# Ten instead of eight heads of an output projection in seven products, two weight sums spread over the pair stage, and the last store on a second queue

## The chip, the cores and the metric

The kernel runs on one core of a Trainium2 chip. The metric is the device time of one execution in microseconds (us), the median of several runs. Engines are named as the profile names them: PE multiplies matrices (PEld loads its weights), DVE is the vector engine, ACT the scalar engine, POOL the GpSimd engine, and SP issues most of the transfers.

## The reference

One layer of a hybrid decoder trunk over 16 meta tokens and 512 tokens of width 2048. The normalised input goes through one projection; its columns feed six gated DeltaNet heads, five GLA heads and five forgetting-attention ("fox") heads, all 128 wide on the value side. The gated head outputs are put side by side (768 + 640 + 640 = 2048) and go through one output projection, then the residual and a final RMSNorm:

```
o_fox = o_fox.reshape(fz.shape) * jax.nn.silu(fz)
o = jnp.concatenate([o_dn, o_gla, o_fox], axis=-1)[:, PAD:].astype(x.dtype)
return x + o @ w_out
...
return rms_norm(h, final_norm_w)[:, N_META:]
```

The change concerns `x + o @ w_out`: 512 tokens, sixteen heads of 128 as the inner dimension, 2048 columns. Everything is float32.

## The kernel before

**Precision.** A float32 product is made of three products of rounded parts: each operand is split into a high part (a cast on ACT, L165 for weights, L1360 and L1370 for activations) and a low part (a subtraction on DVE, L166 for weights, L624 for activations). So each block of a product takes three matmuls: high by high, high by low, low by high. A load of 128x1024 weights (512 KB) is done by `load_half`: a transfer into a `raw` buffer (L147), then the split into `whi` and `wlo`. Two buffers of each rotate.

**Order.** The program is written with a scheduler that orders each engine's instructions ahead of the run by a simulated time and by priorities; on the chip each engine then works through its list in order. A dependency marked `NoSync` only orders the lists; one marked `Sync` also makes the instruction wait on the chip. The weight splits have the highest priority. `paced(x)` lets `x` follow the latest weight split in the order, without a wait.

**Stages.** (1) Input projection of the DeltaNet, GLA and first fox columns, with the token mixers between its matmuls. (2) The *pair stage*: for the last fox heads two column blocks at a time are projected by seven products (`inproj_pair`, L571, seven weight loads for each of seven pairs), with the attention of the preceding head between them (scores L1219 and L1220, softmax L1223 to L1234, transposes L1237, values L1267 to L1271). (3) The output projection (`mms`, matmuls at L1392), which also hides the attention of the last fox head (head 4).

**Output projection.** The heads are numbered 0 to 15: six DeltaNet, five GLA, five fox. The first `SH` = 8 are taken in four pairs. A pair is a 2 x 2 product: two halves of the tokens by two heads, times two heads by two halves of the columns. It is done by seven products of half size instead of eight, in the way of Strassen and Winograd. The seven operands of a pair are `a11`, `a12`, `s2`, `s1`, `s3`, `s4` and `a22`, each 128 x 512 with its two heads' token halves summed as needed. `first_sums` makes `s1` and `s3` on POOL (L634, L635), `differences` (L1434) and L1464 make `s2` and `s4` on DVE, and `operand` splits each one into its high and low part. One operand of one pair needs one load of 512 KB of weights and 12 matmuls of 128x512. Four of the seven weights are sums of blocks of `w_out`, held in DRAM in `tw`. The other `NP` = 8 heads (`plain`) are multiplied in the usual way, in twos: `run` takes two heads and 512 columns, with one load and 24 matmuls.

The order of stage 3 is:

- `pa`: for three blocks of 512 columns (`cc` 0 to 2), the first `EARLY` = `NP - 2` plain heads, `EARLY // 2` runs per block. Between the runs one entry at a time is taken from a list of steps: splitting the plain heads' outputs (`split_o`, from `zrow` or a `zp` row), `load_zr` (L1345, the pairs' outputs from DRAM), `first_sums`, then the operands. `begin` loads x into the accumulators `acc` through POOL's queue (L1386).
- the seven products, `pq`, `pr`, `ps`, over all pairs in turn, on four PSUM banks each. The first uses the pool `psb`, the second the pool `psm`, which the last fox head's attention uses too. `take` adds the results to `acc` on DVE (L1407).
- `pt`: the last two plain heads for `cc` 0 to 2, the first two of the last block's six (`LAST` = `NP - 6` = 2) in one more run, and then, token block by token block, six plain heads of the last column block with weights loaded beforehand by `load_last` (`wl`). After each token block follow the norm, the scaling by row (L1577 on ACT for `cc` 0 and 2, L1579 and L1581 on DVE) and four stores of 256 KB each (L1582).

**Chores.** The summed weights for the pair stage (`ti`) and for the output projection (`tw`) are made by transfers from DRAM to DRAM on POOL's queue: a plain copy (L492) or an accumulating copy (L490). They stand in a list `chores`, each `yield`ing a cost of 1 for a copy and 1.6 for a sum. Every `load_half` adds `rate` to `due` and takes chores while `due` is above zero. One entry of `AHEAD` sets the rate to 1.4 and enters seven groups of jobs for `ti`, and behind them the groups for `tw`, one per pair of heads:

```
AHEAD = {(0, -1): (1.4, (-1, -2, -3, -4, -5, -6, -7), (0, 1, 2, 3))}
...
due[0] += rate[0]
while due[0] > 0 and chores:
    cost = next(chores[0], None)
```

A group has four copies and four sums; for several groups, all copies come first, then the first two sums of each group (into `tw[j, 0]` and `tw[j, 2]`), then the third of each (`tw[j, 1]`), then the fourth of each (`tw[j, 3]`). `fetch` (called after products of the last pair) brings the plain heads' outputs from DRAM into `zrow`.

Of the kernel before, what the change touches and what calls it, by code (L numbers as in the profile page):

```python
# [14 lines left out]
ALU = mybir.AluOpType  # L15
# [3 lines left out]
P = 128  # L19
# [11 lines left out]
LOW = -87.0  # L31

DN_HEADS, GLA_HEADS, FOX_HEADS = 6, 5, 5
SH = 8
NK = 8
H1 = 1
SKIP = 1
# [45 lines left out]
def tile_hybrid_trunk(ctx, tc, xT, xtok, mtok, w_gate, w_in, w_out, w_dn, consts, lmask, fin_w, out, dbg=None):  # L83
    nc = tc.nc
# [12 lines left out]
    def row(name, dt=F32):  # L97
        return wk.tile([P, 3 + T], dt, tag="row", bufs=7, name=name)
# [4 lines left out]
    V, A, G, PE = nc.vector, nc.scalar, nc.gpsimd, nc.tensor  # L103
# [66 lines left out]
    pace, splits, heads_, waits = [None, None], [], [], []  # L170

    def paced(*ins):

        for x in ins:
            tc.add_manual_dep(x.ins, pace[x.ins.engine == pace[1].engine].name, mybir.DependencyInfo(
                mybir.DependencyClass.NoSync, mybir.DependencyReason.DATA), reason="paced")
# [16 lines left out]
    def part(name, n=512):  # L193
        return hp.tile([P, T], F32R, tag="x", name=name)[:, :n]
# [29 lines left out]
    head = {}  # L224
# [254 lines left out]
    ti = drp.tile([len(PAIRS), 4, P, KC], F32, name="ti")  # L479
    tw = drp.tile([SH // 2, 4, P, 1024], F32, name="tw")  # L480
    zd = drp.tile([DN_HEADS + GLA_HEADS + FOX_HEADS - 1, P, S], F32, name="zd")
# [3 lines left out]
    def steps_of(jobs):  # L485

        nonlocal ready
        for kind, out_, in_ in jobs:
            if kind:
                paced(G.dma_start(out=out_, in_=in_, accum_op=ALU.add, max_dma_last_dim=2048))  # L490
            else:
                x = G.dma_start(out=out_, in_=in_)  # L492
                paced(x)
                if ready < 4:
                    ready += 1
                    tc.add_manual_dep(x.ins, maxes[0].name, mybir.DependencyInfo(
                        mybir.DependencyClass.NoSync, mybir.DependencyReason.DATA), reason="behind")
            yield 1.6 if kind else 1
# [14 lines left out]
    def jobs(*groups):  # L513

        for st in range(4):
            for g_ in groups:
                chores.append(steps_of(g_[st]))
# [85 lines left out]
    def conv_silu(key, blk, dst, meta=True):  # L603
# [8 lines left out]
        for w in range(1, 4):  # L612
# [9 lines left out]
             + [("fz", h) for h in range(FOX_HEADS)])  # L622
    heads = heads[:SH] + heads[11 : 11 + F1] + heads[SH:11] + heads[11 + F1 :]
    sub = lambda o, a, b: V.tensor_tensor(out=o, in0=a, in1=b, op=ALU.subtract)  # L624
    pairs = range(SH // 2)
    t0, t1 = slice(0, 256), slice(256, 512)
# [515 lines left out]
            V.memset(first_[n][:, 0:1], 0.0)  # L1142

    def fetch(i):
        if i < 6:
            if i % 3 == 0:
                zrow.append(six.tile([P, 3, S], F32, tag="six", name=f"zp{i}"))
            paced(nc.sync.dma_start(out=zrow[-1][:, i % 3], in_=zd[SH + i]))

# [123 lines left out]
            nc.sync.dma_start(out=zd[DN_HEADS + GLA_HEADS + h], in_=z)  # L1273


    AHEAD = {(0, -1): (1.4, (-1, -2, -3, -4, -5, -6, -7), (0, 1, 2, 3))}
    XSUM = {1: (0, 1, 2), 2: (3, 4, 5), 3: (6, 7)}
    MIX = 10
    PM, SP = (308, 340), (8, 11)
# [1 line left out]
    def ahead(g, i):  # L1281
        for n in AHEAD.get((g, i), ()):
            if isinstance(n, tuple):
                jobs(*[in_jobs(-k - 1) if k < 0 else out_jobs(k) for k in n])
            else:
                rate[0] = n
# [52 lines left out]
    def load_zr():  # L1339

        for i in range(SH):
            if i % 2 == 0:
# [3 lines left out]

    plain = heads[SH:]
    NP = len(plain)
    EARLY, LAST = NP - 2, NP - 6
    oparts = {}  # L1350

    def split_o(i):
        z = zs[plain[i]]
        if i < 6:
            z = zrow[i // 3][:, i % 3]
        elif i < NP - 1:
            z = row(f"zp{i}")[:, :S]
            nc.sync.dma_start(out=z, in_=zd[SH + i])
        hi, lo = part(f"oh{i}"), part(f"ol{i}")
        made = A.copy(hi, z), sub(lo, z, hi.bitcast(F32))  # L1360
        if i > 1:
            paced(*made)
        oparts[i] = hi, lo
# [26 lines left out]
    def mms(p_, o, w, s, first, last):  # L1390
        for n, (o_, w_) in enumerate(((o[0], w[0]), (o[0], w[1]), (o[1], w[0]))):
            mm = PE.matmul(p_, o_[:, s], w_, start=(first and n == 0), stop=(last and n == 2), skip_group_check=True)  # L1392
            order.append(mm.ins)
# [11 lines left out]
    def add(tb, cc, p_, c=slice(0, 512), op=ALU.add):  # L1405
        a = acc[tb, cc][:, c]
        V.tensor_tensor(out=a, in0=a, in1=p_[:, c], op=op)  # L1407
# [4 lines left out]
    def square(tb, cc, c=slice(0, 512), n=0):  # L1412
        sq = row(f"sqf{tb}{cc}{n}")
        A.activation(sq[:, c], acc[tb, cc][:, c], AF.Square, accum_out=ss[:, tb, cc + n : cc + n + 1])  # L1414
# [16 lines left out]
    def differences():  # L1431
        for j in pairs:
# [3 lines left out]
            r["s2"] = r["a11"]  # L1436

    rest = lambda a, b: [split_o(i) for i in range(a, b)]
    steps = [lambda a=a: rest(a, min(a + 2, EARLY)) for a in range(2, EARLY, 2)] + [load_zr]
    steps.append(lambda: (first_sums(), rest(EARLY, EARLY + 1)))  # L1440
# [85 lines left out]
    for c in range(4):  # L1526
        f = part(f"fw{c}").bitcast(F32)
# [20 lines left out]
    for tb in range(4):  # L1548
        cuts = 2 if tb == 3 else 1
        for n in range(cuts):  # L1550
            c = slice(0, 512) if cuts == 1 else slice(CUT, 512) if n else slice(0, CUT)
            p_ = psm.tile([P, 512], F32, tag="m", name="pz") if n else pa[tb]
            for i in range(LAST, NP):
                mms(p_[:, c], oparts[i], [t[:, c] for t in wl[i]], slice(tb * P, (tb + 1) * P),
                    (n == 1 or LAST == 0) and i == LAST, i == NP - 1)
            add(tb, 3, p_, c)
            if n < 1:
                square(tb, 3, c, n)
                if tb == 3:
                    r = rr[:, tb : tb + 1]  # L1560
                    V.reduce_sum(r, ss[:, tb, :4], axis=mybir.AxisListType.X)
                    V.tensor_scalar(r, r, 1.0 / D, EPS, ALU.mult, ALU.add)
        r = rr[:, tb : tb + 1]
        if tb < 3:
            V.reduce_sum(r, ss[:, tb, :4], axis=mybir.AxisListType.X)
            V.tensor_scalar(r, r, 1.0 / D, EPS, ALU.mult, ALU.add)
        else:
            a = acc[tb, 3][:, c]
            V.tensor_tensor_reduce(out=row("sqz")[:, c], in0=a, in1=a, scale=1.0 / D, scalar=r, op0=ALU.mult,
                                   op1=ALU.add, accum_out=rr[:, 4:5])  # L1570
            r = rr[:, 4:5]
        A.activation(r, r, AF.Ln)
        A.activation(r, r, AF.Exp, scale=-0.5)
        for cc in (0, 1, 2, 3):
            a = acc[tb, cc]
            if cc % 2 == 0:
                A.activation(a, a, AF.Copy, scale=r)  # L1577
            elif cc == 3:
                V.scalar_tensor_tensor(out=a, in0=a, scalar=r, in1=fw[cc], op0=ALU.mult, op1=ALU.mult)  # L1579
            else:  # L1580
                V.tensor_scalar_mul(a, a, r)  # L1581
            nc.sync.dma_start(out=out[tb * P : (tb + 1) * P, cc * 512 : (cc + 1) * 512], in_=a)  # L1582


def _layout(x, meta_tokens, norm_w, w_in, conv_w, a_log, dt_bias, dn_norm_w, w_gk2, b_gk,
# [57 lines left out]
```

## Time and profile before

| What | Value |
|---|---|
| median of three runs (lowest, highest) | 1000.51 us (999.34, 1000.78) |
| the profiled execution: its time, its span | 997.56 us, 995.9 us |
| granted PE clock, mean | 0.997 |
| instructions | 19769 |
| POOL busy | 249.0 us, 25% |
| moved by DMA | 186.05 MB, mean 187 GB/s |

Busy times are sums over the span. Matmuls overlap each other in the pipeline, so that the duration of one (about 0.39 us for 128x512) is longer than its share of the time; the spacing is read from a chain or from the start times of a row of them. In the chain of waits, a row is: start, length, what. In groups of instructions the two numbers behind the bar are busy time in us and the mean of one in ns. In the timeline, the brackets give the idle time before an instruction and what ended it.

### The profile page before, as it was taken

The numbers are of one execution on the slowest core, as the hardware profiler recorded it, in microseconds if no ns is written. First come the engines' busy times: TensorE is split into PE (matmuls) and PEld (weight loads), VectorE is DVE, ScalarE is ACT, GpSimd is POOL, SyncE is SP. The second block draws the span as 40 slices with busy tenths as digits, with TensorE's granted clock in tenths as the row PEclk, the third lists the DMA queues.
The fourth block names the chain that finished last, engine by engine and source line by source line (L and its number), as shares of the span: only waits on it lengthen the run. The fifth ranks groups of instructions, "written<-read, shape, count | busy, mean of one in ns | idle before, by whom it ended". The sixth has DMA issues, their size and how long they took to land.

```text
span 995.9 us, 19769 instructions
## 1 busy us (share of the span) xinstructions
PE 980.4 (98%) x7774; PEld 896.6 (90%) x7774; DVE 666.8 (67%) x1443; ACT 475.3 (48%) x1043; POOL 249.0 (25%) x293
## 2 busy tenths in 40 slices
PE   9999999999999999999999999999999999999996
PEld 7899999899999888899999988799999998888885
DVE  6356786966567895434675847776766676877573
ACT  7653533334456234334546444555555554454353
POOL 0031423322233244301313223221221134000060
PEclk9999999999999999999999999999999999999998
DMA  9754666777547688844847866565454577355634
GB/s 346 263 193 168 210 216 238 172 181 173 116 113 169 140 215 198 298 130 144 209 143 190 186 178 178 176 200 161 168 172 135 182 267 273 106 190 199 202 106 169
DMA packets 67489, 186.05 MB, mean 187 GB/s; under 512 B 13725, under 2 KB 16973, under 8 KB 66692
## 3 DMA queue, kind: packets, MB, share of 16 engines
q1 hardware_dynamic: 41920, 121.86, 36.0%
q0 software_dynamic: 16576, 56.83, 23.9%
q10 hardware_dynamic: 8900, 6.10, 2.2%
q8 instruction: 61, 1.00, 0.4%
q14 instruction: 32, 0.26, 0.1%
HBM read 174.07 MB, written 56.69 MB: 232 GB/s over the span
## 4 chain that ended last, share of the span: by engine, by line
PE 70%; DVE 7%; DMA 5%; ACT 3%; issue 2%; POOL 1%; ACTq 0%; DVEq 0%; POOLq 0%
PE pp L240 28%; PE pp_a L571 8%; PE pa L1392 5%; PE pq L1392 4%; PE pt L1392 4%; PE ps L1392 2%; PE pp_b L571 2%; PE pp_d L571 2%; PE pp_c L571 2%; DVE wlo L166 2%; DMA sc<-ab 1%; DMA zd<-gqk 1%; PE pr L1392 1%; PE pss L1041 1%; ACT whi L165 1%
## 5 line engine op out<-in xcount | busy, mean ns | idle before, releaser
L240 PE MATMUL pp<-xh,wlo 128*128 128x264 f32 (+2 forms) x1120 | 272.9, 306 | 2.2 <-DVE wlo L166 2.2
L240 PE MATMUL pp<-xh,whi 128*128 128x264 f32 (+2 forms) x1120 | 273.9, 306 | 0.0
L240 PE MATMUL pp<-xl,whi 128*128 128x264 f32 (+2 forms) x1120 | 272.9, 306 | 0.0
L165 ACT CAST whi<-raw 128x1024 fp32r<-128x1024 f32 x131 | 137.1, 1047 | 157.0 <-PE pp L240 81.2
L166 DVE TENSOR_TENSOR wlo<-raw,whi 128x1024 fp32r<-128x1024 f32 x131 | 160.6, 1226 | 72.8 <-ACT whi L165 64.2
L240 PEld LDWEIGHTS pp<-xh,wlo 128*128 128x128 f32 x1120 | 182.6, 189 | 12.1 <-DVE wlo L166 3.6
L240 PEld LDWEIGHTS pp<-xh,whi 128*128 128x128 f32 x1120 | 182.6, 189 | 9.4 <-ACT whi L165 0.4
L240 PEld LDWEIGHTS pp<-xl,whi 128*128 128x128 f32 x1120 | 182.7, 189 | 8.9 <-issue 0.4
L385 POOL TENSOR_SCALAR stc<-cv 128x528 f32<-128x528 f32 (+1 forms) x18 | 28.9, 1607 | 144.9 <-DVE cv L613 124.4
L613 DVE SCALAR_TENSOR_TENSOR cv<-pb,cpk,cv 128x528 f32<-128x528 f32 (+1 forms) x54 | 41.1, 761 | 0.8
L1417 POOL TENSOR_TENSOR acc<-acc,fw 128x512 f32<-128x512 f32 x4 | 5.8, 1483 | 117.4 <-ACT sqf L1414 117.4
L571 PE MATMUL pp_a<-t,whi 128*128 128x264 f32 (+1 forms) x224 | 30.5, 284 | 0.0
L1392 PE MATMUL pa<-wloo,oh 128*128 128x512 f32 x72 | 28.7, 398 | 0.0
L571 PE MATMUL pp_a<-xh,whi 128*128 128x264 f32 x112 | 28.4, 288 | 0.0
L571 PEld LDWEIGHTS pp_a<-t,whi 128*128 128x128 f32 x224 | 27.9, 189 | 0.5
L1392 PE MATMUL pa<-whio,ol 128*128 128x512 f32 x72 | 28.4, 394 | 0.0
L571 PE MATMUL pp_a<-xl,whi 128*128 128x264 f32 x112 | 28.3, 287 | 0.0
L385 POOL TENSOR_SCALAR stdz<-zdz 128x512 f32<-128x512 f32 x6 | 11.3, 1885 | 62.1 <-DVE zdz L403 62.0
L165 ACT CAST whis<-raws 128x1024 fp32r<-128x1024 f32 x16 | 16.3, 1048 | 21.2 <-PE pq L1392 10.8
L166 DVE TENSOR_TENSOR wlos<-raws,whis 128x1024 fp32r<-128x1024 f32 x16 | 19.2, 1223 | 10.7 <-ACT whis L165 10.6
L1392 PE MATMUL pa<-whio,oh 128*128 128x512 f32 x72 | 26.0, 400 | 0.0
L740 DVE TENSOR_TENSOR ab<-ab 51x30 f32<-51x30 f32 (+14 forms) x60 | 21.2, 354 | 6.4 <-DMA ab<-scr 4.2
(509 smaller groups left out, 2138.6 us busy)
## 6 DMA issues: line engine op xcount, KB each, us to landing
raw<-in_w_in SPq DMA_DIRECT2D x103, 512.0 KB, 3.7
ti<-in_w_in POOLq DMA_DIRECT2D x42, 512.0 KB, 5.5
raw<-ti SPq DMA_DIRECT2D x28, 512.0 KB, 3.3
tw<-in_w_dn POOLq DMA_DIRECT2D x24, 512.0 KB, 5.9
ti<-ti POOLq DMA_DIRECT2D x14, 512.0 KB, 6.3
rawo<-in_w_out SPq DMA_DIRECT2D x13, 512.0 KB, 3.2
raws<-tw SPq DMA_DIRECT2D x12, 512.0 KB, 3.9
xt<-in_xtok SPq DMA_DIRECT2D x8, 512.0 KB, 8.9
```

What stands on the lines that cost most here:

```text
L165: pace[0] = A.copy(hi, raw).ins
L166: pace[1] = V.tensor_tensor(out=lo, in0=raw, in1=hi.bitcast(F32), op=ALU.subtract).ins
L240: mm = PE.matmul(p_[:, :nt], wt[:, j * m : (j + 1) * m], xx[k][:, t0 : t0 + nt], start=(k == 0 and wt is hi and xx is xh), stop=(k == KT - ...
L385: maxes.append(G.tensor_scalar_max(t, src, LOW).ins)
L571: m = PE.matmul(p_[:, cols], wt[:, j * P : (j + 1) * P], xx[j][part_][:, cols], start=first and i == 0, stop=i == len(todo) - 1, skip_grou ...
L613: V.scalar_tensor_tensor(out=c, in0=pb[:, t0 + w : w + T], scalar=cwc[:, blk, w : w + 1], in1=c, op0=ALU.mult, op1=ALU.add)
L740: V.tensor_tensor(out=t3, in0=a3[:, j + 1 :, j : j + 1].to_broadcast([NN * 4 + H, m, j]), in1=a3[:, j : j + 1, 0:j].to_broadcast([NN * 4 + ...
L1041: mm = PE.matmul(ps[o0 : o0 + n, b * n : b * n + n], kx[rr, k0 : k0 + n], qx[rr, q0 : q0 + n], start=True, stop=True)
L1392: mm = PE.matmul(p_, o_[:, s], w_, start=(first and n == 0), stop=(last and n == 2), skip_group_check=True)
L1417: G.tensor_tensor(out=acc[tb, cc], in0=acc[tb, cc], in1=fw[cc], op=ALU.mult)
```

## The change

`SH` goes from 8 to 10: five pairs of heads go by seven products, and six heads remain plain (`NP` = 6, `EARLY` = 4, `LAST` = 0). With that:

- `fetch` brings four heads' outputs instead of six, and `split_o` takes those four from `zrow`.
- The groups for `tw` get a fifth pair, and from the second fox head on the rate falls to 0.35. A sum that is issued in the pair stage gets a `Sync` dependency on the latest weight split on DVE, so POOL waits for it on the chip.
- The four column blocks of a token block are scaled and stored in the order 1, 0, 3, 2, and the very last store (token block 3, `cc` 2) goes through ACT's queue instead of SP's.

```diff
-SH = 8
+SH = 10
...
         for kind, out_, in_ in jobs:
             if kind:
-                paced(G.dma_start(out=out_, in_=in_, accum_op=ALU.add, max_dma_last_dim=2048))
+                x = G.dma_start(out=out_, in_=in_, accum_op=ALU.add, max_dma_last_dim=2048)
+                if ("pair", 0) in head:
+                    tc.add_manual_dep(x.ins, pace[1].name, mybir.DependencyInfo(
+                        mybir.DependencyClass.Sync, mybir.DependencyReason.DATA), reason="paced")
+                else:
+                    paced(x)
...
     def fetch(i):
-        if i < 6:
+        if i < 14 - SH:
...
-    AHEAD = {(0, -1): (1.4, (-1, -2, -3, -4, -5, -6, -7), (0, 1, 2, 3))}
+    AHEAD = {(0, -1): (1.4, (-1, -2, -3, -4, -5, -6, -7), (0, 1, 2, 3, 4)), ("f", 1): (0.35,)}
...
     def split_o(i):
         z = zs[plain[i]]
-        if i < 6:
+        if i < EARLY:
             z = zrow[i // 3][:, i % 3]
...
-        for cc in (0, 1, 2, 3):
+        for cc in (1, 0, 3, 2):
             a = acc[tb, cc]
...
-            nc.sync.dma_start(out=out[tb * P : (tb + 1) * P, cc * 512 : (cc + 1) * 512], in_=a)
+            (nc.scalar if tb == 3 and cc == 2 else nc.sync).dma_start(
+                out=out[tb * P : (tb + 1) * P, cc * 512 : (cc + 1) * 512], in_=a)
```

## The prediction

> **What bounds the kernel now.** I read the page first (engine shares, DMA issues), then PE's waits, then the chain of waits from the last pair product to the end.
>
> ```profile
> PE 980.4 (98%) x7774; PEld 896.6 (90%) x7774; DVE 666.8 (67%) x1443; ACT 475.3 (48%) x1043; POOL 249.0 (25%) x293
> ```
>
> PE's waits from 600 us to the end (total, times, longest):
>
> ```profile
> PE pp L240 <- DVE wlo L166: 0.5, 1, 0.5
> PE pss L1041 <- DVE kq L1027: 0.4, 2, 0.2
> ```
>
> The chain, some pieces (start, length):
>
> ```profile
> 814.39 0.13 PE pfa L1219 x2
> ...
> 845.90 12.06 PE pa L1392 x52
> ...
> 869.32 0.46 PE pfo L1270 x2
> 869.78 1.16 PE pa L1392 x5
> 870.94 11.12 PE pq L1392 x48
> ...
> 948.43 37.73 PE pt L1392 x168
> ```
>
> PE waits 0.9 us in the last 396 us, and the whole output projection is PE behind PE. So a matmul taken out is worth its spacing, as long as nothing else becomes late. A 128x512 matmul takes 12.06/52 = 0.232 us in `pa` and 11.12/48 = 0.232 us in the products. In `pt` 96 of them lie between these starts:
>
> ```profile
> 948.27 1.10 PE L1392 MATMUL pt<-whio,oh 128*128 128x512 f32 x4
> ...
> 970.38 0.40 PE L1392 MATMUL pt<-wlh,oh 128*128 128x512 f32 x1
> ```
>
> That is 22.11/96 = 0.230 us.
>
> **Matmuls: -2.7 us.** `pa` goes from nine runs to six: 72 matmuls less, -16.7 us. Seven products get a fifth pair: 84 more, +19.5 us. `pt` loses the run before the last column block: 24 less, -5.5 us. The last token blocks keep their six heads. Together 12 fewer and -2.7 us. All of it lies on PE's path.
>
> **Splits: 0.** Loads of weights (`pa`, products, `pt` with `load_last`) go from 9 + 28 + 7 = 44 to 6 + 35 + 6 = 47.
>
> ```profile
> L165 ACT CAST whis<-raws 128x1024 fp32r<-128x1024 f32 x16 | 16.3, 1048 | 21.2 <-PE pq L1392 10.8 <-PE ps L1392 6.2 <-PE pr L1392 4.2
> L166 DVE TENSOR_TENSOR wlos<-raws,whis 128x1024 fp32r<-128x1024 f32 x16 | 19.2, 1223 | 10.7 <-ACT whis L165 10.6
> L1370 ACT CAST s<-zr 128x256 fp32r<-128x256 f32 x16 | 6.2, 403 | 3.4 <-DVE zr L1434 2.4 <-PE pq L1392 0.5 <-PE pr L1392 0.4
> L624 DVE TENSOR_TENSOR s<-zr,s 128x256 fp32r<-128x256 f32 x16 | 6.3, 420 | 0.0
> L624 DVE TENSOR_TENSOR ol<-zp,oh 128x512 fp32r<-128x512 f32 x7 | 7.6, 1114 | 0.0
> L1407 DVE TENSOR_TENSOR accs<-accs,pq 128x512 f32<-128x512 f32 x12 | 7.8, 682 | 0.0
> ```
>
> A load in a product has 12 x 0.232 = 2.8 us of PE beside it and needs 1.05 us of ACT and 1.22 us of DVE; one operand of one pair adds 0.40 and 0.42 us, and four `take`s of 0.68 us are now shared by five loads instead of four. That is 1.22 + 0.42 + 0.54 = 2.2 us of DVE per 2.8 us, against 2.3 before: PE still covers it. Without that cover each split would cost up to 2.3 us. The casts wait for PE in that row, not PE for them.
>
> **The `pa` stage: 0 to +2.3 us, I take +0.2.** It is here that the cover gets thin. Five stretches of the stage, only the first and their sum:
>
> ```profile
> 814.84:826.00 11.16, 11.16 (x52) 9.15 (x52) 8.64 (x23) 4.69 (x10) 9.12 (x14) 1.00 0.99 351
> ...
> sum 56.10, PE 56.10 PEld 45.88 DVE 41.68 ACT 23.40 POOL 18.74; mean PE 11.22 PEld 9.18 DVE 8.34 ACT 4.68 POOL 3.75
> ```
>
> Of 56.1 us, 216 x 0.232 = 50.1 are `pa` and 6.0 the last head's attention. With 144 the stage lasts 33.4 + 6.0 = 39.4 us and ends at 854.2. DVE had 41.7 us of work there; three splits (-3.7) and two subtractions of plain heads (-2.2) go, two operands (+0.8) and one difference (+0.4) come: 37.0 us in 39.4. But six `s` subtractions (2.5) and the four L1464 (1.4) have until the second product, so 33.1 us must be done, 84%.
>
> The attention is the piece that can be late: it ran from 814.4 to 869.8 (the chain above), and one more DVE step freed its bank at 870.5:
>
> ```profile
> 869.81 0.69 DVE L1271 TENSOR_TENSOR zfz<-pfo,zfz 128x512 f32<-128x512 f32 x1 [1.55 <-PE pfo L1270]
> ```
>
> Now `a11` starts at 854.2 and ends 60 x 0.232 = 13.9 us later, 868.1. The next product needs all four `psm` banks, its fourth bank 9 matmuls (2.1 us) after its start. If the attention keeps its old end, PE waits 870.5 - 870.2 = 0.3 us where the other three banks are free, 2.4 us where the late bank comes first. The scheduler places the attention's steps ahead of operands, so I take 0.2.
>
> Transfers stay: 15 loads of `zp` and `zr` before (7 + 8), 15 after (5 + 10), two of them shifted into the busy stretch above (0.99 of the DMA engines). The first adds need x in `acc`:
>
> ```profile
> 816.66 2.24 POOL L1386 DMA_DIRECT2D acc<-in_xtok  x4
> ...
> DMA to landing us min/median/max: 5.8/7.2/7.6
> ```
>
> The last of four lands at about 818.4 + 7.6 = 826.0. Before, 72 matmuls came ahead of the adds; now 48, and PE asks for the first freed bank at 814.8 + 48 x 0.232 + 0.5 of attention = 826.4, for the fourth 2.1 us later. Two loads more at 351 GB/s are 1.5 us, so 827.5 + 0.7 for the add: just covered, at worst 0.5 us late.
>
> POOL makes two more sums (L634, L635):
>
> ```profile
> 830.23 2.13 POOL L634 TENSOR_TENSOR zr<-zr 128x256 f32<-128x256 f32 x3
> 833.80 2.13 POOL L635 TENSOR_TENSOR zr<-zr 128x256 f32<-128x256 f32 x3
> 833.89 3.67 DVE L166 TENSOR_TENSOR wloo<-rawo,whio 128x1024 fp32r<-128x1024 f32 x1
> ```
>
> A split beside three such sums took 3.67 instead of 1.22 us, 0.8 us per sum. So two sums may cost DVE 1.6 us, and runs of 5.6 us cover that.
>
> **Weight sums in the pair stage: 0, at worst +7.** Costs in the list: seven groups for `ti` at 10.4 (4 + 4 x 1.6) are 72.8, four for `tw` 41.6, together 114.4; five make it 124.8. The loads:
>
> ```profile
> raw<-in_w_in SPq DMA_DIRECT2D x103, 512.0 KB, 3.7
> raw<-ti SPq DMA_DIRECT2D x28, 512.0 KB, 3.3
> tw<-tw POOLq DMA_DIRECT2D x8, 512.0 KB, 7.4
> ```
>
> 131 loads, 49 of them in the pair stage, leave 82 before it: 82 x 1.4 = 114.8. That took all of the old list; of the new one six sums are left (one into `tw[4, 1]`, five into `tw[j, 3]`). At 0.35 one goes per 4 to 5 loads, so they are through after about 24 of 49, long before the products read `tw`. The four copies and two first sums of the fifth pair go at the old rate among the earlier ones, between matmuls of a PE that is 98% busy over the span; I count them at 0, and at the price of the six below if that cover fails.
>
> In the pair stage there was no such traffic. Landings of `raw` there (first fence), and from 592 to 640 us, with sums beside them (second):
>
> ```profile
> DMA to landing us min/median/max: 3.1/3.3/6.7
> ```
>
> ```profile
> DMA to landing us min/median/max: 3.3/4.7/7.1
> ```
>
> Room, from a split and its product:
>
> ```profile
> 805.03 1.05 ACT L165 CAST whi<-raw 128x1024 fp32r<-128x1024 f32 x1 [0.89 <-DMA raw<-ti]
> ...
> 808.70 2.94 PE pp_c L571 x24
> ```
>
> This cast waited 0.89 us for its transfer and still ended 2.6 us ahead. A sum must delay a load by more than that; the medians differ by 1.4. I take 0.
>
> The wait that the change adds stands in POOL's list; behind it queue the scalings (L1181, L1186, L1187), the masks (L1207) and the silu's L385, which the attention needs, and through it PE. POOL already stood 21.2 us at such a split without PE waiting:
>
> ```profile
> POOL fqk L1207 <- DVE wlo L166: 21.2, 2, 17.1
> L490 POOL DMA_DIRECT2D tw<-tw x8: 879/1003/1642, 557.3 to 618.3; - x8
> ```
>
> One issue holds POOL 1.0 us, six times in 170 us.
>
> **Last stores: -0.3 (0 to -0.5).**
>
> ```profile
> 990.04 0.70 ACT L1577 ACTIVATE accs<-accs,frs 128x512 f32<-128x512 f32 x1
> 990.83 0.89 SPq L1582 DMA_DIRECT2D out<-accs  x2
> ...
> L1582 SPq DMA_DIRECT2D out<-accs x12: 332/399/1793, 977.7 to 991.3; - x12
> DMA to landing us min/median/max: 2.7/3.1/4.0
> ```
>
> The last store (`cc` 2) has its tile at 990.74, but SP begins to issue it at 991.3, as the second of that pair. ACT can begin at 990.75, 0.5 us earlier, and then SP's store of 990.8 is last. The new order 1, 0, 3, 2 is the one in which SP already issued them as they came ready, so by itself it moves nothing. If the transfers, not the issues, set the end, the gain is 0. From the row alone it might also be more: landings reach 4.0 us where 2.7 would do, and if SP's own queue made that difference, a second queue would save up to 1.3 us besides. I take -0.3, nearest to the issue's own 0.4, and 0 and -0.5 for the ends.
>
> The Trainium skill ("DMA: Bandwidth & Descriptors", Issuing engines are not separate DMA queues) says that transfers issued from different engines end on the same 16 DMA engines, so that a second issuer saves only the time of issuing. By it nothing of the 1.3 us comes back and the sum would stand at -0.4 for this part at most; no run so far has two issuers for these stores, so the trace cannot yet say.
>
> **Sum.** -2.7 + 0.2 - 0.3 = -2.8 us. The profiled execution took 997.6 us, its span 995.9 and 1.7 around it; it becomes 994.8. It stood 2.9 below the median of the runs, 1000.5, for which I forecast 997.7.
>
> **Rivals.**
>
> *The attention keeps its end and PE waits at the bank change.* For it: the attention's pace is set by DVE, not by PE's share. Against: 84% is not full, and its steps go ahead of operands in the order. With 2.4 instead of 0.2: -0.6 us, 999.9, no measurable change.
>
> *DVE becomes the bound of the shorter `pa` stage.* In the last block of the attention, between the exponential and the scaling of its result, lie these:
>
> ```profile
> 849.04 0.19 ACT L1229 ACTIVATION_READ_ACCUMULATOR fp<-fp,fsm 128x1 f32 x1
> ...
> 855.17 0.48 DVE L1234 TENSOR_SCALAR fp<-fp,fsm 128x512 f32<-128x512 f32 x1
> ```
>
> 5.9 us went to operands and adds queued between. Operands now come earlier, into the blocks before it. If one more block loses 5.9 us, the attention ends at 876.4, PE waits 876.4 - 870.2 = 6.2 us at the bank change, and the net is -2.7 - 0.3 + 6.2 = +3.2: 1003.7. It is slower by over 0.2% from an end at 875.2 on. Against: the order is planned anew, and 33 us of needed work fit.
>
> *The thin sums delay the pair stage.* If all six make a load land in 7.1 instead of 3.3 us, 3.8 less the room of 2.6 is 1.2 us each, 7.2 in all: +4.4, 1004.9. It decides when landings pass 5.9 us. Against: most room is larger, and a sum meets two or three loads only.
>
> *The second queue gives nothing* is the end 0 of that term, inside the forecast.
>
> **How the numbers follow.** A measurement of this kernel tells about 0.2%, 2.0 us, from no change. Forecast 0.60, bank change 0.18, DVE 0.14, sums 0.08. Faster by over 0.2% (below 998.5) is the forecast, 0.60; within, the bank change, 0.18; slower, the other two, 0.22. The forecast's own range is 996.5 to 998.5: its terms give -3.2 to -2.0, and below that 0.8 for the spread of the runs. With the bank change that holds 0.78; the DVE case enters at 1002.5, so the range goes to 1002.6.
>
> **What would show it.** Right: 7762 matmuls; chain pieces of `pa` with 144, of the products with 420, of `pt` with 144; ten `tw<-tw`, the last near 710 to 730 us; no PE wait over 0.5 us; the last store issued by ACT. Wrong: a PE wait at `pr` or at `pp_a` to `pp_d`, or a `pfx` or `pfo` that PE waits for; DVE above 95% in the 40 us of `pa`; `raw` landing beyond 6 us; or waits in the first 600 us, where I expect none beyond today's.

## Result and profile after

The changed kernel took 1006.09 us (median of eleven runs, 1004.03 to 1015.03), the kernel before on the same chip 999.44 us. The ratio is 1.0082 [1.0053, 1.011]: slower by about 0.8%, where I had forecast 997.7 us, faster. Ratios leave out executions in a slower state of the chip: one of four of the denser list below, and one of eight of the last experiment.

The first profile is of the longest of the eleven runs (1015.03 us). The first experiment gave a second one, of a run of 1003.71 us; sizes are read from that where the two differ. Engine lines, first profile, then second:

```profile
PE 984.5 (97%) x7762; PEld 897.9 (89%) x7762; DVE 672.6 (66%) x1452; ACT 480.3 (47%) x1051; POOL 258.8 (26%) x303
```

```profile
PE 981.7 (98%) x7762; PEld 895.9 (89%) x7762; DVE 668.7 (67%) x1452; ACT 479.8 (48%) x1051; POOL 260.0 (26%) x303
```

There are 12 matmuls fewer, as forecast. PE's waits (total, times, longest), first profile, then second:

```profile
PE pa L1397 <- DVE wloo L166: 5.2, 1, 5.2
PE pwg L957 <- DVE zsdz L859: 2.7, 1, 2.7
...
PE pt L1397 <- ACT whio L165: 1.1, 1, 1.1
...
PE pp_a L576 <- ACT vf L590: 1.0, 1, 1.0
```

```profile
PE pwg L957 <- DVE zsdz L859: 2.3, 1, 2.3
...
PE pp_a L576 <- ACT vf L590: 1.0, 1, 1.0
...
PE pq L1397 <- ACT whia L165: 0.8, 1, 0.8
PE pq L1397 <- DVE accs L1412: 0.7, 1, 0.7
```

None of these stood in the profile before. Two lie ahead of the output projection (`pwg` near 498 us, `pp_a` near 652 us), where I expected nothing. The wait of 5.2 us in `pa` came in one profile only.

The next rows are windows (stretch, length, busy time and count of PE, PEld, DVE, ACT, POOL, granted clock, DMA share, GB/s): `pa`, the products and `pt` of the second profile, then of the kernel before.

```profile
819.30:856.66 37.36, 37.36 (x174) 30.38 (x174) 26.94 (x63) 16.16 (x34) 20.88 (x30) 1.00 0.79 287
856.66:958.57 101.91, 100.23 (x435) 80.73 (x433) 73.75 (x109) 47.89 (x71) 0.00 (x0) 1.00 0.53 181
958.57:991.77 33.20, 32.89 (x146) 26.65 (x144) 23.94 (x36) 18.19 (x47) 18.53 (x12) 1.00 0.36 119
```

```profile
814.59:870.77 56.18, 56.18 (x259) 45.97 (x259) 41.76 (x90) 23.40 (x50) 18.99 (x28) 1.00 0.58 210
870.77:948.27 77.50, 77.50 (x338) 63.25 (x336) 55.81 (x73) 34.96 (x45) 0.00 (x0) 1.00 0.58 197
948.27:986.01 37.74, 37.74 (x170) 31.37 (x169) 23.66 (x39) 19.91 (x48) 17.79 (x12) 1.00 0.33 112
```

The second span is 5.7 us longer than before (1001.6 - 995.9). Of that 4.7 us lie ahead of the start of `pa` (819.30 - 814.59) and 1.0 behind it, where I had summed -2.8. Thirteen matmuls of the attention moved from `pa` into the first product; they take 2.3 us (0.23 + 1.36 + 0.22 + 0.46 in the chain of the repaired kernel below). With them `pa` came out as forecast: 37.4 + 2.3 = 39.7 us against 39.6. The products did not: 101.91 - 77.50 = 24.4 us, less these 2.3, is 22.1 instead of 19.5. `pt` gave 4.5 instead of 5.5 us.

### The profile page after: what moved, and what is told of

It is laid out like the page before. It is cut to its first block, busy times and chain, and to the rows that moved or that the text cites. A ratio compares the mean times of both kernels' runs of the same rounds, so it can differ in the third digit from the quotient of the medians.

```text
span 1013.0 us, 19798 instructions
## 1 busy us (share of the span) xinstructions
PE 984.5 (97%) x7762; PEld 897.9 (89%) x7762; DVE 672.6 (66%) x1452; ACT 480.3 (47%) x1051; POOL 258.8 (26%) x303
## 4 chain that ended last, share of the span: by engine, by line
PE 65%; DMA 8%; DVE 7%; issue 4%; ACT 3%; POOL 2%; ACTq 0%; POOLq 0%; DVEq 0%
PE pp L240 28%; PE pp_a L576 7%; PE pq L1397 5%; PE pt L1397 3%; PE ps L1397 3%; PE pp_c L576 2%; DMA xb<-in_xT 2%; PE pp_d L576 2%; PE pa L1397 2%; DMA sc<-ab 2%; PE pp_b L576 1%; DVE wlo L166 1%; PE pr L1397 1%; DMA rawo<-in_w_out 1%; PE pss L1046 1%
## 5 line engine op out<-in xcount | busy, mean ns | idle before, releaser
L166 DVE TENSOR_TENSOR wlos<-raws,whis 128x1024 fp32r<-128x1024 f32 x20 | 24.1, 1222 | 15.6 <-ACT whis L165 15.6
L165 ACT CAST whis<-raws 128x1024 fp32r<-128x1024 f32 x20 | 20.6, 1048 | 28.5 <-PE pq L1397 11.4
L1397 PE MATMUL pq<-whia,a 128*128 128x512 f32 x80 | 26.1, 397 | 1.4 <-DVE accs L1412 1.0
L1397 PE MATMUL pq<-whis,s 128*128 128x512 f32 x80 | 25.3, 394 | 0.0
L1397 PE MATMUL ps<-whis,s 128*128 128x512 f32 x80 | 25.3, 393 | 0.0
```

Of the source, the lines that this page charges most:

```text
L165: pace[0] = A.copy(hi, raw).ins
L166: pace[1] = V.tensor_tensor(out=lo, in0=raw, in1=hi.bitcast(F32), op=ALU.subtract).ins
```

## Experiments

Two groups of theories: *traffic* (the fifth group's copies and sums cost time ahead of the output projection) and *output* (the output projection's shorter `pa` no longer covers what surrounds it). A ratio is to the kernel before on the same chip; that kernel's medians differ between chips (998.4 to 999.6 us), so kernels from different experiments are compared by how far each stands above it.

**The change again.**

> The changed kernel once more, for a second profile. In the profile of its first runs PE waited 2.7 us at pwg for zsdz (GLA stage) and 5.2 us at pa for the split wloo (first output blocks). If these two waits belong to the kernel, both come again, within 1 us of those sizes, and the ratio to the kernel before is 1.005 to 1.011. If they belong to that one execution, at least one of them is under 1 us here and the loss is spread over many places.

1005.95 us, 1.0063 [1.0041, 1.0085]. The `pwg` wait came again (2.3 us), the `pa` wait did not: that one belongs to some executions. The spread runs from 1003.7 to 1009.7 us.

**Stores alone.**

```diff
-        for cc in (0, 1, 2, 3):
+        for cc in (1, 0, 3, 2):
...
+            (nc.scalar if tb == 3 and cc == 2 else nc.sync).dma_start(...)
```

> The kernel before with the last stores alone as in the change (order 1, 0, 3, 2, the last one issued by ACT). My prediction's term: -0.3 us (0 to -0.5), 999.1 us. Rival (transfers set the end): 0. Either way under what the times can tell; the span from pz's last start to the end tells them apart: 8.05 us before, 7.7 by the prediction, 8.05 by the rival.

1000.33 us, 1.0008 [0.9994, 1.0021]: not to be told from no change in the time. The place shows a little: from the first matmul of `pz` (988.98, before 986.01) to the end it took 9.66 instead of 9.84 us.

**The fifth group moved wholly into the pair stage.**

```diff
-    AHEAD = {(0, -1): (1.4, (...), (0, 1, 2, 3, 4)), ("f", 1): (0.35,)}
+    AHEAD = {(0, -1): (1.4, (...), (0, 1, 2, 3)), ("f", 1): (0.35, (4,))}
```

> The changed kernel, but the early list holds the old four groups of tw at 1.4, and the whole fifth group (four copies, four sums) goes through the pair stage at 0.35. Theory GLA (the longer list's copies delay the loads of x that x_sums makes on the same queue, so DVE is held at xa and PE at pwg, and PE runs slower for some us after that wait): the pwg wait goes, 4 to 6 us come back, about 1001 us. Theory pa (the loss comes from the burst of zr loads and sums in the shortened pa stage): unchanged within 1 us, about 1006. Theory pair stage (thin sums delay the pair's loads): 1 to 3 us slower than the changed kernel, since more of them stand there.

1007.92 us, 1.0087 [1.0066, 1.0108]. The `pwg` wait went, but the time did not follow: it is 2 us above the change on the same chip, as the third theory had it, and in the profile the pair stage is 1.4 us longer (178.0 against 176.6).

**Loads of `zr` spread.**

```diff
-            nc.sync.dma_start(out=zs[heads[i]], in_=zd[i])
+            paced(nc.sync.dma_start(out=zs[heads[i]], in_=zd[i]))
...
+    steps = [lambda: (rest(2, EARLY), load_zr(0, 1)), lambda: load_zr(1, 3),
+             lambda: (load_zr(3, 5), first_sums(range(3)))]
```

> The changed kernel, but the ten zr loads are spread over the runs of the pa stage between the loads of weights (one, two and two pairs), and POOL's sums follow in two portions. Theory pa (eight zr loads in one burst ahead of a load of weights make it land 13.4 us after issue, and a split beside six POOL sums takes 5.9 us): the wait of 5.2 us at pa falls under 1 us and 5 to 6 us come back, about 1000.5 us. Theory GLA: unchanged within 1 us, about 1006.

1004.95 us, 1.0051 [1.0033, 1.0069]: 1 us less than the change on the same chip, which the intervals do not tell from nothing, and not the 5 to 6 of that theory. No wait over 0.6 us in `pa`, yet waits of 2.9 us and 0.9 us at `pp_a`. The burst is not the bulk of the loss.

**POOL's sums on DVE.**

```diff
-            G.tensor_tensor(out=r["s1"], in0=r["a22"], in1=r["a21"], op=ALU.subtract)
-            G.tensor_tensor(out=r["s3"], in0=r["a11"], in1=r["a21"], op=ALU.subtract)
+            paced(sub(r["s1"], r["a22"], r["a21"]), sub(r["s3"], r["a11"], r["a21"]))
```

> The changed kernel, but the ten sums of the pa stage (s1, s3 of five pairs) are made by DVE instead of POOL. Theory output part (the second profile shows 0 us of wait in pa but 2.0 us at the first product's splits and 0.4 in pt, and the first profile a split of 5.9 us beside six POOL sums): if the sums beside splits are the cause, 1 to 3 us come back, 1003 to 1005. Theory traffic (the loss comes from the fifth group's copies and sums ahead of the output projection): unchanged, 1006; DVE has 4.2 us more work in pa, so by my rival that DVE bounds this stage it is up to 4 us slower.

1017.79 us, 1.0191 [1.0157, 1.0225]: far outside both. DVE's timeline shows why:

```profile
837.10 1.10 DVE L629 TENSOR_TENSOR zr<-zr 128x256 f32<-128x256 f32 x3 [2.80 <-DMA zr<-zd]
...
840.68 0.76 DVE L629 TENSOR_TENSOR zr<-zr 128x256 f32<-128x256 f32 x1 [1.55 <-DMA zr<-zd]
```

The sums do not cost DVE much (0.4 us each), but DVE stands at them for the transfers of `zr`, and the adds that free PE's banks and the attention stand behind. On POOL the same wait holds nobody up.

**The fifth group left out.**

```diff
-    product(pa, "s2", lambda j: tw[j, 1], False, True)
+    product(pa, "s2", lambda j: tw[min(j, 3), 1], False, True)
```

(so for the four products that read `tw`; the list as in the kernel before)

> The changed kernel with the old early list of four groups: the fifth group's four copies and four sums are left out, and the fifth pair's products read the fourth pair's sums. All matmuls, splits and loads are as in the change. Theory traffic: the 4.7 us that the second profile lost before the output projection go, about 1001 us (the +1.0 of its output projection stays). Theory order (the loss in those stages comes from the new places of buffers and steps, not from the traffic): 1004 to 1006.

1002.79 us, 1.0048 [1.0023, 1.0074], between the two: 3.6 us above the kernel before (1002.79 - 999.2), where the change stood 6.7 above it. No `pwg` wait, and `pp_a` 0.2 us.

**The fifth group added to the kernel before.**

```diff
-    AHEAD = {(0, -1): (1.4, (...), (0, 1, 2, 3))}
+    AHEAD = {(0, -1): (1.4, (...), (0, 1, 2, 3, 4)), ("f", 1): (0.35,)}
```

(and, as in the change, the `Sync` dependency of the sums in the pair stage; a fifth place in `tw` is filled from old blocks, and nothing reads it)

> The kernel before with the fifth group's four copies and four sums added to its early list just as in the change, thin sums and their waits included; nothing reads the result, and the output projection is unchanged. Theory traffic: 3.5 to 6 us slower than the kernel before, about 1004. Theory order: within 1 us of the kernel before.

1001.5 us, 1.0027 [1.0008, 1.0047]: 2.3 us, less than forecast but in that direction. The two kernels together nearly close the account: 2.3 for the group, 3.6 for all else (the kernel without it), 5.9 of the 6.7 us between 999.44 and 1006.09. Each of the two is known to some 2 us only.

**A denser list, no thin sums.**

```diff
-    AHEAD = {(0, -1): (1.4, (...), (0, 1, 2, 3, 4)), ("f", 1): (0.35,)}
+    AHEAD = {(0, -1): (1.53, (...), (0, 1, 2, 3, 4))}
```

> The changed kernel with the early list at 1.53 units a load instead of 1.4, so that all five groups are through before the pair stage, and no thin sums. Theory pair stage (of the loss, the 1.5 to 2 us of the pair stage come from thin sums beside its loads): those go, 1004 to 1004.5. Theory that traffic costs the same wherever it stands: unchanged, 1006, the GLA stage up to 2 us longer instead.

1012.58 us over all four executions (1011.63 over the three that the ratio counts), 1.0135 [1.0111, 1.0158]. Neither theory had this: 9% more chores per load are dearer than the thin sums that they replace. The profile is of the execution left out, so no cause is read from it.

**Thin sums held back to the second pair head.**

```diff
-    ("f", 1): (0.35,)}
+    ("f", 1): (0,), ("f", 2): (0.35,)}
```

> The changed kernel with one edit: no thin sums in the first pair head, where the last loads of x go through the same queue; they start with the second. Theory traffic at x (the sums make these loads land late, ACT stands at xe, and the evacuation vf that PE's pp_a needs stands behind it): the pp_a waits of 1.0 to 2.9 us fall to 0.2 or less and 1 to 2.5 us come back, about 1004. Rival (the waits come from the new order of buffers): pp_a waits stay, 1006.

1009.83 us, 1.0108 [1.0081, 1.0135], no gain and probably a loss. The `pp_a` wait stayed at 0.9 us in a profile of 1003.2 us, which is the shortest of its six runs; where the others lost 6 us more no profile shows. So the wait does not need the thin sums; on this the rival (the new order) came out. What the sums in flight have to do with it is taken up below.

**Repairs of the output projection.** On top of the spread loads: operands after `a11` made inside the first products, and of the product loads that go to the spare buffers (every third) the last moved from the 33rd to the 34th of 35, so that it is again the second last (it was the 27th of 28).

```diff
-    steps += [lambda: operand("a11"), lambda: operand("a12"), differences, lambda: operand("s2"), ...]
+    hooks = {("a11", 1): lambda: operand("a12"), ("a11", 2): differences, ("a11", 3): lambda: operand("s2"), ...}
...
-        if nw[0] < 0 or nw[0] % 3:
+        if nw[0] not in (*range(3, 31, 3), 34):
```

> The changed kernel with the three repairs of the output projection alone (zr spread, operands after a11 into the products, weight loads of pt as early as before). Theory output (in the profiles of the change its output projection, from the first pa to the end, takes 182.3 to 189.4 us against 181.3 before, of which 2 us are waits at the first product's second and third split, 0.3 to 1.5 at pt's second, and 0 to 5.2 in pa): it falls to 178.5 to 180 us, and the time to 1002 to 1003. Rival (the stage is full and something else becomes late): 182 or more, 1005.

1001.85 us, 1.004 [1.002, 1.0061]: 3.1 us above the kernel before on that chip, where the change stood 6.7 and 6.3 above it. Its three windows:

```profile
820.18:858.51 38.33, 37.49 (x174) 30.11 (x174) 25.66 (x64) 15.27 (x32) 19.70 (x30) 1.00 0.78 281
858.51:958.25 99.74, 99.72 (x433) 81.00 (x434) 74.76 (x110) 48.12 (x73) 0.00 (x0) 1.00 0.55 190
958.25:990.62 32.37, 32.37 (x145) 26.85 (x144) 20.91 (x37) 19.31 (x47) 16.52 (x12) 1.00 0.35 115
```

Products and `pt` are 2.2 and 0.8 us shorter than in the second profile of the change, without a wait. From `pa` to the end it took 180.1 us, against 181.3 before. Of the three repairs only the spread loads were run alone; what each of the other two gave is read from the place of the waits.

**The same without the fifth group.**

> The changed kernel with the output repairs and without the fifth group's copies and sums (the fifth pair's products read the fourth pair's sums). These are the conditions under which my forecast summed: matmuls -2.7 us and nothing late. If the sum is right and only its covers failed: 996.5 to 998 us. If the matmuls themselves cost more than their spacing before (0.232 against 0.2305 us in the products): 999 or more.

999.34 us, 1.0008 [0.999, 1.0026]. That is no measurable change, short of the 996.5 to 998 of the forecast's sum and within the second theory's range. That theory's cause is there but small: in the products a matmul takes (99.74 - 2.27)/420 = 0.2321 us, against 77.50/336 = 0.2307 before, 0.6 us over all of them. From `pa` to the end it took 180.2 us, the same as its sister.

**All repairs and the held sums.**

> The changed kernel with all repairs: zr loads spread and POOL's sums in two portions; the operands after a11 moved from the end of pa into the first two products, behind a split each; one load of the last product put on another buffer, so that the weight loads of pt come as early as before; and the thin sums held back until the second pair head, past the last loads of x. If each of these waits is a cost of its own, their gains add: about 2 us in the pair stage, 4 in the output projection, so 1000 us. If PE's loss only moves to the next late step, 1003 or more.

1006.2 us, 1.007 [1.0049, 1.009]. Holding the sums back spoils the gain of the repairs here too. In its profile (1005.27 us) `pa` took 40.9 us, where the repairs alone had 38.3, and PE waited 2.0 us there, by the profile for the attention's exponential on ACT (`fp`, L1234); why the held sums bring that is not shown.

**The whole fifth group from the second pair head on**, with the output repairs, then with POOL's sums in the first product besides, then without any repair.

```diff
-    (0, 1, 2, 3, 4)), ("f", 1): (0.35,)}
+    (0, 1, 2, 3)), ("f", 2): (0.35, (4,))}
```

> The kernel of the output repairs, with the whole fifth group (copies and sums) only from the second pair head on, past the last loads of x; up to there the list is that of the kernel before. Theory traffic at x: no pp_a wait, pair stage 175 to 176 us, time as without the fifth group: 998.5 to 1000. Rival (the fifth group's bytes cost 2 to 3 us wherever they stand): pair stage 177.5 or more, 1001 to 1002.

> As the kernel before this one, and POOL's ten sums moved from the pa stage into the first product. Theory sums (a split beside them takes up to 5.9 instead of 1.2 us, so pa loses 1 to 2 us even when the loads come in time): pa 37.1 to 37.5 us instead of 38.3, and time 1 us less than the kernel before this one. Rival (the exponential on ACT holds the split in pa, and the sums now hold the splits of the first product): pa 38.3, products longer by 1 us or more.

> The change with that one edit: the whole fifth group from the second pair head on. Theory traffic at x: the time of the kernel without the fifth group, 1002.5 to 1003.5 us. Rival (bytes cost wherever they stand): 1005 to 1006.

1001.07 us (1.0018 [0.9997, 1.0038]), 1003.64 us (1.0049 [1.0027, 1.0072]) and 1004.57 us (1.0057 [1.0032, 1.0081]). The first is the best version with ten heads that computes everything; it does not beat the kernel before. The third is no better than the change. The copies did not stay past the loads of x: with no wait of their own they were planned at 646 to 648 us, still in the first pair head, and ACT then stood for a weight load beside them:

```profile
646.16 1.09 POOL L497 DMA_DIRECT2D tw<-in_w_dn  x2
647.48 0.97 POOL L497 DMA_DIRECT2D tw<-in_w_dn  x2
```

```profile
655.18 1.05 ACT L165 CAST whi<-raw 128x1024 fp32r<-128x1024 f32 x1 [6.01 <-DMA raw<-ti]
```

In all three profiles PE then waited 1.2 us in sum for the next copies out of its banks (`vf`, L594). So the edit was not the clean test that I meant. Sums in the first product made `pa` longer (41.7 us instead of 38.6), against the expectation: on DVE a split now stood ahead of the reciprocal of the attention's last block, and PE waited 2.9 us for that block.

Lengths from one profile each, in us, between the first matmuls of the stages (the last column from the first of `pt` to the end of the span):

| kernel | to pair stage | pair stage | `pa` | products | `pt`, end |
|---|---|---|---|---|---|
| before | 639.4 | 175.2 | 56.2 | 77.5 | 47.6 |
| before, new stores | 641.0 | 175.5 | 57.2 | 77.5 | 47.4 |
| before, with fifth group | 636.9 | 178.3 | 56.1 | 77.5 | 47.6 |
| change, first profile | 646.4 | 177.2 | 44.1 | 101.3 | 44.0 |
| change, second profile | 642.7 | 176.6 | 37.4 | 101.9 | 43.1 |
| fifth group in pairs | 641.2 | 178.0 | 37.2 | 101.7 | 43.7 |
| `zr` spread | 640.9 | 180.5 | 38.3 | 102.2 | 43.9 |
| POOL's sums on DVE | 644.9 | 178.9 | 49.5 | 102.4 | 44.1 |
| no fifth group | 640.6 | 175.6 | 38.6 | 102.2 | 43.3 |
| thin sums held | 638.5 | 178.0 | 38.4 | 102.2 | 44.0 |
| output repairs | 641.6 | 178.6 | 38.3 | 99.7 | 42.0 |
| output repairs, no fifth group | 643.5 | 175.4 | 38.4 | 99.7 | 42.1 |
| output repairs, thin sums held | 642.9 | 178.3 | 40.9 | 99.4 | 42.0 |
| group from second head, repairs | 642.2 | 176.4 | 38.6 | 99.7 | 42.0 |
| the same, sums in the products | 638.8 | 177.6 | 41.7 | 99.6 | 42.0 |
| group from second head alone | 641.0 | 177.1 | 37.4 | 102.1 | 43.4 |

The first column scatters by several us between kernels with the same list, so little is read from it. The second separates: 176.4 us or more with the fifth group, 175.2 to 175.6 without. (The denser list has the whole group ahead of the pair stage; its profile, 175.0 us there, is left out as said.)

## Why the prediction was wrong, step by step

The second profile lies some 8.5 us from my sum (+5.7 instead of -2.8): 4.7 ahead of `pa`, 2.6 in the products, 1.0 in `pt`, 0.3 at the last stores.

**Weight sums in the pair stage, "0".** This step failed, above all in its second half, where I counted the fifth pair's copies and first sums "among the earlier ones" at 0. I compared the six sums with the room of the pair's weight loads, and named a delay of those as the rival (1004.9 us, chance 0.08); PE waited for none of those loads in either profile of the change. What became late was something that I did not list: the last four loads of x (`xe`), issued on POOL's queue. ACT's timeline in the first pair head, kernel without the fifth group, then the change (second profile):

```profile
644.79 0.52 ACT L553 ACTIVATE xe<-xe,cpk 128x264 f32<-128x264 f32 x1 [0.38 <-DMA xe<-in_xT]
646.91 0.52 ACT L553 ACTIVATE xe<-xe,cpk 128x264 f32<-128x264 f32 x1 [1.61 <-DMA xe<-in_xT]
...
648.59 0.37 ACT L590 COPY vf<-pp_a 128x264 f32<-128x264 f32 x1
```

```profile
648.62 0.52 ACT L553 ACTIVATE xe<-xe,cpk 128x264 f32<-128x264 f32 x1 [2.72 <-DMA xe<-in_xT]
649.98 0.52 ACT L553 ACTIVATE xe<-xe,cpk 128x264 f32<-128x264 f32 x1 [0.85 <-DMA xe<-in_xT]
...
651.65 0.37 ACT L590 COPY vf<-pp_a 128x264 f32<-128x264 f32 x1
```

ACT takes its list in order, so the copy that empties PE's bank stands behind the scaling of x, and PE behind that. At this copy PE waits 0 us in the eight profiles without the group in the early list, and 0.9 to 2.9 us in the eight with it at the rate of 1.4. The pair stage is 1.3 to 5.3 us longer than before in the profiles with the group. So the cover that I named ("between matmuls of a PE that is 98% busy") does not exist for an engine that stands at a transfer.

How the group does this is shown in part. It is not a sum in flight beside these loads. POOL's queue and SP's, before, then first profile of the change:

```profile
640.42 2.88 POOL L546 DMA_DIRECT2D xe<-in_xT  x4 [13.64 <-DVE xl L554]
642.04 0.33 SPq L147 DMA_DIRECT2D raw<-in_w_in  x1
```

```profile
635.94 0.98 POOL L490 DMA_DIRECT2D tw<-tw  x1
647.90 2.93 POOL L551 DMA_DIRECT2D xe<-in_xT  x4 [10.98 <-DVE xl L559]
648.28 0.33 SPq L147 DMA_DIRECT2D raw<-in_w_in  x1
...
652.06 0.98 POOL L490 DMA_DIRECT2D tw<-tw  x1
```

The sum ahead of the loads of x landed 4.9 us before the first of them went out, the next one was issued behind the last, and with the thin sums held back there is none for another 27 us; the wait was there all the same. What differs is the place of a weight load of SP: it follows the first load of x by 0.4 us in all eight profiles with the wait, by 1.6 to 1.9 us in those without, and that load of x lands 4.4 to 4.6 us after its issue instead of 3.1 to 3.3. So the longer list moved the loads against each other. Whether the group's transfers or the newly planned order of the lists did that, no run separates.

Ahead of the pair stage stands the `pwg` wait: DVE stood 6.3 us for the scaled `xa` (4.3 before) with `zsdz` behind it. The load of `xa` landed 5.5 us after its issue (3.5 before), with three copies of the list issued behind it within 2 us, where the kernel before has two. The wait came in both profiles of the change and in two others with this list (2.2 and 0.6 us); in the other four the load landed in 3.6 to 3.8 us behind the same three copies, and PE did not wait. So I do not count it to every run. Its price is more than the 2.3 us of the wait: behind it PE ran at half its clock (last section).

**Products, "PE still covers it".** This step failed at the start of the first product. The count (2.2 us of DVE per 2.8) holds in the middle of the products, which run without a wait. But `pa` is 19 us shorter, and ACT's casts for `a11` and `a12`, behind a late row of a plain head (`zp`), end up in one block ahead of the second split:

```profile
853.57 0.62 ACT L1365 CAST oh<-zp 128x512 fp32r<-128x512 f32 x1 [1.10 <-DMA zp<-zd]
854.10 3.17 ACT L1375 CAST a<-zr 128x256 fp32r<-128x256 f32 x10
857.17 0.47 ACT L1246 CAST fphi<-pfx 128x384 fp32r<-128x384 f32 x1
857.54 1.06 ACT L1267 CAST ptm<-pfw 32x128 fp32r<-32x128 f32 x4
858.62 2.00 ACT L165 CAST whia<-rawa 128x1024 fp32r<-128x1024 f32 x2
```

PE waits 0.8 us for this split. Its next wait, 0.7 us, is for an add on DVE (`accs`) that frees a bank, behind the low parts and differences of the same operands:

```profile
859.31 1.09 DVE L629 TENSOR_TENSOR a<-zr,a 128x256 fp32r<-128x256 f32 x3
...
861.33 0.68 DVE L1412 TENSOR_TENSOR accs<-accs,pa 128x512 f32<-128x512 f32 x1
```

Ten heads have ten such casts where eight had eight, but they need not lie there: with all operands after `a11` made inside the products both waits are gone, and the repaired kernel's products are 2.2 us shorter. My rival "DVE becomes the bound" named the crowding on DVE, but at the attention and with 6 us, and it had nothing of ACT.

**`pt`, -5.5.** Mis-sized by 1.0: PE waits 0.3 to 1.2 us at the second run's `whio`. The loads of SP, before, then second profile of the change:

```profile
936.97 0.33 SPq L147 DMA_DIRECT2D rawo<-in_w_out  x1
942.43 0.33 SPq L1399 DMA_DIRECT2D rawl<-in_w_out  x1
945.23 0.33 SPq L147 DMA_DIRECT2D rawo<-in_w_out  x1
```

```profile
949.97 0.33 SPq L147 DMA_DIRECT2D rawo<-in_w_out  x1
952.77 0.33 SPq L1404 DMA_DIRECT2D rawl<-in_w_out  x1
959.25 0.33 SPq L147 DMA_DIRECT2D rawo<-in_w_out  x1
```

Before `pt` began (948.27) both loads of `rawo` had been issued; now the second follows its start (958.57). Every third product load takes a spare buffer, and 35 loads end on another beat of that count than 28. With one such load moved by one place (among the repairs), the second `rawo` is issued at 955.37, ahead of that kernel's `pt` (958.25), and `pt` takes 32.4 us, 5.4 less than before: the term as forecast.

**`pa`, "+0.2".** Right in the second profile, but 6.8 us longer in the first (44.12 - 37.36). There, the fourth `rawo` landed so late that its split met six sums on POOL (first profile; then the fourth split of the second):

```profile
841.95 5.93 DVE L166 TENSOR_TENSOR wloo<-rawo,whio 128x1024 fp32r<-128x1024 f32 x1 [5.39 <-ACT whio L165]
```

```profile
842.10 1.41 POOL L639 TENSOR_TENSOR zr<-zr 128x256 f32<-128x256 f32 x2
843.48 2.76 POOL L640 TENSOR_TENSOR zr<-zr 128x256 f32<-128x256 f32 x4
```

```profile
834.05 1.23 DVE L166 TENSOR_TENSOR wloo<-rawo,whio 128x1024 fp32r<-128x1024 f32 x1 [1.52 <-ACT whio L165]
```

I had 0.8 us per sum and "runs of 5.6 us cover that". The price holds (5.93 - 1.22 = 4.7 us for six), but the cover is the time by which the split is early, and a late load takes that away first. How often this happens I cannot say; the runs of 1009 us and more may be such, which no profile shows. After the repairs `pa` takes 38.3 us; 38.3 + 2.3 is 1.0 over my 39.6, and 0.8 of it is a wait that the profile puts down to the attention's exponential on ACT (`fp`, L1234).

**Last stores, -0.3.** In the kernel before alone it was -0.2 at its place. In the change nothing of it was left (9.87 us from `pz` to the end): DVE still scaled the token block before, and the last norm began 0.2 us later behind `pz`. The repaired kernel had the gain again (9.67). By the Trainium skill ("DMA: Bandwidth & Descriptors", Issuing engines are not separate DMA queues) a second issuer saves only issue time; the -0.2 agree, being less than the 0.4 us of one issue.

**Matmuls, -2.7.** Nearly right once their covers were restored: products 99.7 - 2.3 - 77.5 = 19.9 instead of 19.5, `pt` -5.4 instead of -5.5. In the change itself the waits ate more than the 2.7. Even under the conditions of my sum the output projection gained 1.1 us (180.2 instead of 181.3), not 2.8: 1.0 us are the remainder in `pa`, 0.5 the products, the rest `pt` and the stores. The median there came out at no change (from 1.0 us below to 2.6 above). That profile reached the pair stage 4.1 us later than the kernel before with the same list; why stays open.

## What to carry to other kernels

A count of matmuls is the smallest part of such a change: here 2.7 us stood against more than 8 lost elsewhere. For each added transfer, list what else goes through the same queue and which in-order engine stands at those transfers, not only the loads that PE needs; an entry in a planned list also moves its neighbours. When a stage that hides preparation is shortened, lay the preparation out anew, and check the beat of any rotation of buffers.

## What the hardware showed

After a wait PE also runs on at half its clock, which I had not priced. First profile, behind the wait at `pa` (it ended at 847.93):

```profile
847.90:850.90 3.00, 2.97 (x8) 2.49 (x9) 2.28 (x6) 1.74 (x3) 0.00 (x0) 0.50 0.51 175
850.90:853.90 3.00, 3.00 (x14) 2.41 (x14) 1.74 (x7) 1.88 (x4) 0.00 (x0) 0.99 0.52 173
```

Six matmuls fewer in 3 us (8 instead of 14) are another 1.4 us on top of the 5.2. The Trainium skill ("TensorE: Matmul & The Clock Gate", What's actually happening) gives half rate after an idle window of about 3.4 us; here the row after the wait of 2.7 us at `pwg` shows 0.50 as well, so a shorter wait was enough, and the measurement decides:

```profile
500.50:503.20 2.70, 2.70 (x13) 2.67 (x13) 1.61 (x5) 1.03 (x2) 0.00 (x0) 0.50 0.82 258
```

In this profile the clock stood at 0.50 from 499.4 to 506.2 us; in the second one, behind a wait of 2.3 us, from 500.3 to 503.6. There a pair of matmuls of 128x264 began every 0.44 us instead of 0.24, which by my estimate (3.3 us at that pace) costs another 1.5 us. The length of the wait alone does not decide it: behind one of 2.4 us at `pp_a`, in the profile of the output repairs, the clock stayed at 1.00.
